# First row tile's scores by one 256-column matmul per component, and four moved positions in the order of the last two heads

## The chip, the cores and the metric

The kernel runs on one core of one Trainium2 chip. The metric is the device time of one execution in microseconds (us). Names of engines: PE is TensorE (matmuls), PEld its weight loads, DVE is VectorE, ACT is ScalarE, POOL is GpSimd, SP is SyncE, which only issues transfers.

## What is computed

One decoder block over 512 tokens of width 1024, in float32: differential attention with 8 heads (two score components of 64 dimensions each per head) beside a causal pooling branch, a gated merge, an output projection, and an MLP with squared ReLU. The change touches the attention scores:

```python
for i in range(S // Q_BLOCK):                 # four row tiles of 128 queries
    q0 = i * Q_BLOCK
    kend = q0 + Q_BLOCK
    s = jnp.einsum('bqhcd,bkhcd->bhcqk', qb, kb)          # c: two components
    s = jnp.where(mask, s, -jnp.inf)                      # causal
    p = jax.nn.softmax(s, axis=-1)
    w = p[:, :, 0] - lam * p[:, :, 1]
    outs.append(jnp.einsum('bhqk,bkhd->bqhd', w, vb))
```

Row tile i has 128 queries and (i + 1) * 128 keys, so the first row tile has 128 keys only.

## The kernel before

Everything is laid out with 128 partitions. Each float32 operand of a matmul is kept as a rounded high part and a low remainder (type fp32r), and a product is summed from the parts that matter. For the scores the high part of q and its remainder stand together in `qs[:, c]` (64 partitions each), the high part of k in `kz[:, c]` with the other 64 partitions zero, and `ks[:, c]` has k's remainder in one half and k's high part in the other. A row tile's scores of a component are then two matmuls with the same stationary operand, `qs` against `ks` (line 395) and `qs` against `kz` (line 396), summed in one PSUM bank.

The work goes in this order: the value projection (to 56 us), the eight heads (`attn`, 57 to 305 us), the output projection and the MLP. Within the heads the program calls `attn(h)`, then the q and k projection of the next head (`qk`), then some "fillers": input projections of the pooling branch (`pool(g)`, names u0 to u3) and of the gates (`gate`, names ga0 to gp7), and the merges. Every projection is 24 matmuls of 512 columns (`mm3`, lines 131, 132 and 135). Its sum lies in one of three PSUM banks, used in turn (`acc`); a new projection or pooling product (`pp`, lines 485 to 489) can start in a bank when DVE has read the bank's last sum. So u3, which comes three uses behind gp5 (gp5, pp4, pp5, u3), starts behind the DVE instruction that reads gp5 (line 474).

For each row tile of a head: scores (lines 395, 396), on DVE a mask with a row minimum (397), on ACT two exponentials (401), on DVE a reciprocal and a scaling (403, 404), on ACT a scaling (405), on DVE the difference of the components (406), on PE the transposes of the result (410), and then two copies into the buffer `wt` (412, 413). When all four row tiles are in `wt`, twelve matmuls multiply it by the values (418, called PV here). There is one `wt`, so that a head's copies wait for the PV matmuls of the head in front. Score banks are two, used in turn (`sbk`), and so are the banks of the transposes (`tbk`).

The program is not run in the order in which it is written: a scheduler with a cost model sorts the instructions of each engine ahead of time, within the dependencies. `after(later, earlier)` adds a dependency that holds `later` behind `earlier` in that order, with no semaphore. On the chip each engine takes its instructions strictly in that order.

Of the kernel before, what the change touches and what calls it, by code (L numbers as in the profile page):

```python
# [12 lines left out]
F32R = mybir.dt.float32r  # L13
I32 = mybir.dt.int32
AF = mybir.ActivationFunctionType
ALU = mybir.AluOpType
AX = mybir.AxisListType

P = 128
S = 512  # L20
D = 1024
NK = D // P
H = 8
# [4 lines left out]
NEG = -3.0e38  # L28
# [23 lines left out]
def block_kernel(ctx, tc, xT, x_tok, gains, pos, consts, w_in, w_v, w_pool, w_out, w_up, w_dn, out):  # L52
    nc = tc.nc
    V, A, G, T = nc.vector, nc.scalar, nc.gpsimd, nc.tensor
    EXPLN = "natural_log_exp_and_others"

    def after(later, earlier):
        tc.add_manual_dep(
            later.ins, earlier.ins.name,
            mybir.DependencyInfo(mybir.DependencyClass.NoSync, mybir.DependencyReason.DATA), reason="issue order",  # L60
        )

    state = {}
# [4 lines left out]
    cf = ctx1.enter_context(tc.tile_pool(name="cf", bufs=1))  # L68
    tp = ctx1.enter_context(tc.tile_pool(name="tp", bufs=1))
# [17 lines left out]
    def tmp(tag, name, shape=(P, S), dt=F32, bufs=2):  # L87
        return tp.tile(list(shape), dt, tag=tag, name=name, bufs=bufs)

    def f(ap):  # L90
        return ap.bitcast(F32)
# [35 lines left out]
    def mm3(acc, hi, lo, rh, rl):  # L127

        for k in range(NK):
            c = slice(k * P, (k + 1) * P)  # L130
            T.matmul(acc, lhsT=hi[:, c], rhs=rh[:, k, :], start=k == 0, stop=False)  # L131
            T.matmul(acc, lhsT=hi[:, c], rhs=rl[k], start=False, stop=False)  # L132
        for k in range(NK):
            c = slice(k * P, (k + 1) * P)
            T.matmul(acc, lhsT=lo[:, c], rhs=rh[:, k, :], start=False, stop=k == NK - 1)  # L135
# [19 lines left out]
    ident = cp.tile([P, P], F32, name="ident")  # L155
# [6 lines left out]
    mask = cf.tile([P, S], F32, name="mask")  # L162
# [15 lines left out]
    rb = cf.tile([P, S], F32, name="rb")  # L178
# [38 lines left out]
    for n in range(2):  # L217
        accs = [bank((0, 1, 2, 3, 4, 5, 6, 0)[4 * n + t], f"v{n}_{t}") for t in range(NT)]
        for kk in range(4):
# [24 lines left out]
            if n == 0 and 0 < kk < 3:  # L244
                i = kk - 1
# [111 lines left out]
    def proj(m, name, eng=None):  # L357
        hi, lo = get_w(w_in[m], name, eng)
        a_ = acc(name)
        mm3(a_, hi, lo, xh, xl)  # L360
        return a_

    lo_, hi_ = slice(0, 64), slice(64, 128)

    kzs = [cf.tile([P, 2, S], F32R, name=f"kz{i}") for i in range(2)]
    for kz in kzs:
        G.memset(f(kz)[hi_, 0, :], 0.0)
        G.memset(f(kz)[lo_, 1, :], 0.0)

    def qk(h):  # L370
        qs = tp.tile([P, 2, S], F32R, tag="qs", name=f"qs{h}", bufs=2)
        ks = tp.tile([P, 2, S], F32R, tag="ks", name=f"ks{h}", bufs=2)
        kz = kzs[h % 2]
        q = rope(proj(h, f"q{h}", V) if h else q0, f"q{h}")
        for c, own, oth in ((0, lo_, hi_), (1, hi_, lo_)):
            A.copy(out=qs[own, c, :], in_=q[own])
            V.tensor_tensor(out=qs[oth, c, :], in0=q[own], in1=f(qs)[own, c, :], op=ALU.subtract)
        k = rope(proj(8 + h, f"k{h}", V), f"k{h}")
        for c, own, oth in ((0, lo_, hi_), (1, hi_, lo_)):
            A.copy(out=kz[own, c, :], in_=k[own])  # L380
        for c, own, oth in ((0, lo_, hi_), (1, hi_, lo_)):
            A.copy(out=ks[oth, c, :], in_=f(kz)[own, c, :])
            V.tensor_tensor(out=ks[own, c, :], in0=k[own], in1=f(kz)[own, c, :], op=ALU.subtract)
        return qs, ks, kz

    def attn(h, qs, ks, kz):
        wt = wt_all
        for i in range(NT):
            N = (i + 1) * P
            qsl = slice(i * P, i * P + P)  # L390
            pr = tmp(f"p{i}", f"p{h}_{i}", (P, 2, N), bufs=1)
            st = tmp("st", f"st{h}_{i}", (P, 6), bufs=3)
            for c in range(2):
                s_ = sbk(f"s{h}_{i}_{c}")
                T.matmul(s_[:, :N], lhsT=qs[:, c, qsl], rhs=ks[:, c, :N], start=True, stop=False)
                T.matmul(s_[:, :N], lhsT=qs[:, c, qsl], rhs=kz[:, c, :N], start=False, stop=True)  # L396
                V.tensor_tensor_reduce(  # L397
                    out=pr[:, c, :N], in0=s_[:, :N], in1=mask[:, S - N :], scale=-0.125, scalar=-NEG,
                    op0=ALU.add, op1=ALU.min, accum_out=st[:, c : c + 1],
                )  # L400
                A.activation(out=pr[:, c, :N], in_=pr[:, c, :N], func=AF.Exp, scale=-1.0,  # L401
                             bias=st[:, c : c + 1], accum_out=st[:, 2 + c : 3 + c])
            V.reciprocal(out=st[:, 4:6], in_=st[:, 2:4])
            V.tensor_scalar(out=st[:, 5:6], in0=st[:, 5:6], scalar1=lvec, scalar2=None, op0=ALU.mult)
            A.activation(out=pr[:, 1, :N], in_=pr[:, 1, :N], func=AF.Copy, scale=st[:, 5:6])
            V.scalar_tensor_tensor(out=pr[:, 0, :N], in0=pr[:, 0, :N], scalar=st[:, 4:5], in1=pr[:, 1, :N],
                                   op0=ALU.mult, op1=ALU.add)
            t_ = tbk(f"t{h}_{i}")
            for j in range(i + 1):
                T.transpose(out=t_[:, j * P : j * P + P], in_=pr[:, 0, j * P : j * P + P], identity=ident)  # L410
            tv = t_[:, :N].rearrange("p (j q) -> p j q", q=P)
            A.copy(out=wt[:, 0, : i + 1, qsl], in_=tv)
            V.tensor_tensor(out=wt[:, 1, : i + 1, qsl], in0=tv, in1=f(wt)[:, 0, : i + 1, qsl], op=ALU.subtract)
        o_ = obk(f"o{h}")
        n = 0
        for vv, ww in ((vh, 0), (vl, 0), (vh, 1)):
            for j in range(NT):
                T.matmul(o_[:, j * P :], lhsT=vv[:, h, j * P : j * P + P], rhs=wt[:, ww, j, j * P :], start=n == 0, stop=n == 11,  # L418
                         skip_group_check=True)
                n += 1  # L420
        o = tmp("o", f"o{h}", bufs=2)
        A.copy(out=o, in_=o_)
        sqh = tmp("sqh", f"sqh{h}", dt=F32R, bufs=1)
        A.activation(out=sqh, in_=o_, func=AF.Square)
        sql = tmp("y", f"sql{h}", dt=F32R, bufs=1)
        sq = tmp("sq", f"sqo{h}")
        (V if h == H - 1 else G).tensor_tensor(out=sq, in0=o, in1=o, op=ALU.mult)
        (V if h == H - 1 else G).tensor_tensor(out=sql, in0=sq, in1=f(sqh), op=ALU.subtract)
        ss = obk(f"ss{h}")
        T.matmul(ss, lhsT=onesr, rhs=sqh, start=True, stop=False)  # L430
        T.matmul(ss, lhsT=onesr, rhs=sql, start=False, stop=True)
        y = tmp("y", f"y{h}", bufs=1)
        rsqrt(y, ss, sq, P)
        if h == H - 1:
            return o, y
        V.scalar_tensor_tensor(out=o, in0=o, scalar=subc, in1=y, op0=ALU.mult, op1=ALU.mult)
        return o, None

    def pool(g):
        w = WINDOWS[g]  # L440
        a_ = proj(24 + g, f"u{g}", "dma")
        pad = tmp("u", f"u{g}", (P, 16 + S), bufs=1)
        G.memset(pad[:, :16], 0.0)
        u = pad[:, 16:]
        V.tensor_tensor(out=u, in0=a_, in1=rb, op=ALU.mult)
        bufs_ = [tmp("pa", f"pa{g}", (P, 16 + S), bufs=1), tmp("pb", f"pb{g}", (P, 16 + S), bufs=1)]
        for b_ in bufs_[:g]:
            G.memset(b_[:, :16], 0.0)
        cur, s_ = pad, 1
        n = 0  # L450
        while s_ < w:
            nxt = bufs_[n % 2]
            G.tensor_tensor(out=nxt[:, 16:], in0=cur[:, 16:], in1=cur[:, 16 - s_ : 16 + S - s_], op=ALU.add)
            cur, s_, n = nxt, 2 * s_, n + 1
        win = cur[:, 16:]
        d = bufs_[n % 2][:, 16:]
        V.scalar_tensor_tensor(out=d, in0=win, scalar=1.0 / w, in1=u, op0=ALU.mult, op1=ALU.subtract)
        V.tensor_tensor(out=d[:, :w], in0=win[:, :w], in1=rcc[:, :w], op=ALU.mult)
        V.tensor_tensor(out=d[:, :w], in0=d[:, :w], in1=u[:, :w], op=ALU.subtract)
        dh = tmp("dh", f"dh{g}", dt=F32R, bufs=1)  # L460
        dl = tmp("dl", f"dl{g}", dt=F32R, bufs=1)
        A.copy(out=dh, in_=d)
        V.tensor_tensor(out=dl, in0=d, in1=f(dh), op=ALU.subtract)
        wr = tmp("wpr", f"wpr{g}", (P, 256), bufs=1)
        after(nc.sync.dma_start(out=wr, in_=w_pool[:, g, :]), state["x"])
        wph = wt_all[:, 0, 2, 0:256]
        wpl = wt_all[:, 1, 2, 0:256]
        A.copy(out=wph, in_=wr)
        V.tensor_tensor(out=wpl, in0=wr, in1=f(wph), op=ALU.subtract)
        return dh, dl, wph, wpl  # L470

    def gate(m, name, dst):
        a_ = proj(m, name, "dma")
        V.tensor_tensor(out=dst, in0=a_, in1=rb, op=ALU.mult)

    def merge(h, sg, a, sa, sp, dh, dl, wph, wpl):
        a, y = a
# [554 lines left out]
```

## Time and profile before

| | |
|---|---|
| median of 3 runs | 674.83 us (674.45 to 675.34) |
| the profiled execution | 674.09 us, span of the profile 671.9 us |
| PE busy | 663.1 us (99%), 3688 matmuls |
| DVE, ACT, POOL busy | 526.1, 461.0, 112.0 us |
| granted TensorE clock, mean of the core | 0.996 |

The profiled execution is 0.74 us below the median; 2.2 us of it lie outside the span. In the timeline of the profile a row has start, duration, engine, line, operation, the names out<-in, and the shape; the duration of a matmul runs to its modelled end and so overlaps the matmul behind it. What a matmul costs PE is therefore read here from the starts of two rows that follow each other.

### The profile page before, as it was taken

The page shows a single profiled execution, that of the slowest core. Times are in us where ns is not written, and L with a number is a line of the kernel's source. Part 1 is how long each engine was busy: PE and PEld are TensorE (multiplying, and loading weights), DVE is VectorE, ACT ScalarE, POOL GpSimd, SP SyncE. Part 2 cuts the span into 40 slices and gives each one's busy share as a digit, 9 for nine tenths or more (in the row PEclk, how much of TensorE's full clock was granted, in tenths as well). Part 3 has the DMA queues.
Part 4 walks back from the last instruction along what each step waited for, and adds up shares of the span by engine and source line. Part 5 has one row for each costly group of instructions (what it writes and reads, how often), then busy time and mean ns, then how long its engine had stood idle before and what let it go on. Part 6 is the DMA issues. An engine that isn't in the chain of part 4 may idle for free.

```text
span 671.9 us, 9994 instructions
## 1 busy us (share of the span) xinstructions
PE 663.1 (99%) x3688; PEld 579.6 (86%) x3688; DVE 526.1 (78%) x882; ACT 461.0 (69%) x741; POOL 112.0 (17%) x130
## 2 busy tenths in 40 slices
PE   9999999999999999999999999999999999999995
PEld 7888888888888888888889988999889998899884
DVE  6855977799979986875588998657994599747995
ACT  8465587978887698884477975367743695256974
POOL 2001110142133212520202020202102021210120
PEclk9999999999999999999999999999999999999998
DMA  9416464435263365574976596776959578494863
GB/s 317 162 57 185 126 151 126 103 94 126 87 142 103 98 166 105 126 184 172 312 208 112 159 235 186 167 191 146 236 199 187 193 164 261 117 212 132 214 126 125
DMA packets 32880, 109.34 MB, mean 163 GB/s; under 512 B 4032, under 2 KB 4928, under 8 KB 32832
## 3 DMA queue, kind: packets, MB, share of 16 engines
q0 software_dynamic: 10656, 38.80, 32.3%
q1 hardware_dynamic: 21744, 69.38, 29.3%
q8 instruction: 29, 0.48, 0.3%
q10 hardware_dynamic: 432, 0.52, 0.2%
q14 instruction: 19, 0.16, 0.1%
HBM read 106.59 MB, written 2.10 MB: 162 GB/s over the span
## 4 chain that ended last, share of the span: by engine, by line
PE 98%; DMA 1%; DVE 0%; ACT 0%; issue 0%; SPq 0%
PE um L785 8%; PE um L788 8%; PE um L782 8%; PE dm L875 8%; PE dm L877 8%; PE dm L878 8%; PE v L235 2%; PE o L418 2%; PE ga L132 2%; PE ga L131 2%; PE gp L135 2%; PE gp L132 2%; PE k L132 2%; PE k L131 2%; PE gp L131 2%; PE k L135 2%
## 5 line engine op out<-in xcount | busy, mean ns | idle before, releaser
L877 PE MATMUL dm<-wh_dt,z 128*128 128x512 f32 (+1 forms) x128 | 49.5, 386 | 0.0
L878 PE MATMUL dm<-wl_dt,z 128*128 128x512 f32 (+1 forms) x128 | 49.4, 386 | 0.0
L875 PE MATMUL dm<-wh_dt,z 128*128 128x512 f32 (+1 forms) x128 | 49.0, 387 | 0.0
L785 PE MATMUL um<-gss,wh_ut 128*128 128x256 f32 x192 | 48.2, 283 | 0.0
L782 PE MATMUL um<-gss,wh_ut 128*128 128x256 f32 x192 | 48.0, 283 | 0.0
L401 ACT ACTIVATE p<-p,st 128x128 f32<-128x128 f32 (+3 forms) x64 | 35.7, 558 | 14.1 <-DVE st L397 13.8
L895 DVE TENSOR_TENSOR x<-x,dm 128x512 f32<-128x512 f32 x48 | 32.5, 681 | 16.3 <-PE dm L878 16.3
L112 ACT CAST wh_ut<-wga_uNone 128x1024 fp32r<-128x1024 f32 x24 | 24.9, 1050 | 29.7 <-PE dm L877 19.2
L112 ACT CAST wh_ub<-wr_u 128x1024 fp32r<-128x1024 f32 x24 | 25.1, 1050 | 22.1 <-PE um L785 9.8
L686 POOL DMA_DIRECT2D wga_dNone<-w_dn x16 | 14.2, 885 | 154.2 <-DVE wl_dt L113 154.2
L113 DVE TENSOR_TENSOR wl_ut<-wga_uNone,wh_ut 128x1024 fp32r<-128x1024 f32 x24 | 29.1, 1221 | 13.0 <-ACT wh_ut L112 12.9
L877 PE MATMUL dm<-wh_db,z 128*128 128x512 f32 x96 | 37.2, 389 | 0.0
L878 PE MATMUL dm<-wl_db,z 128*128 128x512 f32 x96 | 37.2, 389 | 0.0
L785 PEld LDWEIGHTS um<-gss,wh_ut 128*128 128x128 f32 x192 | 36.9, 192 | 0.0
L782 PEld LDWEIGHTS um<-gss,wh_ut 128*128 128x128 f32 x192 | 36.8, 192 | 0.0
L875 PE MATMUL dm<-wh_db,z 128*128 128x512 f32 x96 | 35.7, 389 | 0.0
L113 DVE TENSOR_TENSOR wl_ub<-wr_u,wh_ub 128x1024 fp32r<-128x1024 f32 x24 | 29.1, 1219 | 7.4 <-ACT wh_ub L112 7.4
L686 POOL DMA_DIRECT2D wga_uNone<-w_up x18 | 15.6, 865 | 115.8 <-DVE wl_ut L113 81.4
L112 ACT CAST wh_dt<-wga_dNone 128x1024 fp32r<-128x1024 f32 x24 | 24.9, 1049 | 14.4 <-issue 6.7
L755 DVE TENSOR_TENSOR z<-rawz,z 128x1024 fp32r<-128x1024 f32 x28 | 33.6, 1218 | 0.5 <-ACT z L752 0.5
L397 DVE CUSTOM_DVE_ANT_0 p<-s,mask 128x128 f32<-128x128 f32 (+3 forms) x64 | 30.3, 484 | 3.6 <-PE s L396 3.5
L785 PE MATMUL um<-gab,wh_ub 128*128 128x256 f32 x128 | 32.5, 283 | 0.0
(324 smaller groups left out, 2203.3 us busy)
## 6 DMA issues: line engine op xcount, KB each, us to landing
wr_u<-w_up SPq DMA_DIRECT2D x24, 512.0 KB, 5.4
wr_d<-w_dn SPq DMA_DIRECT2D x24, 512.0 KB, 4.2
wga_uNone<-w_up POOLq DMA_DIRECT2D x18, 512.0 KB, 7.2
wga_dNone<-w_dn POOLq DMA_DIRECT2D x16, 512.0 KB, 5.7
wr_k<-w_in SPq DMA_DIRECT2D x8, 512.0 KB, 3.3
wr_ga<-w_in SPq DMA_DIRECT2D x8, 512.0 KB, 3.3
wr_gp<-w_in SPq DMA_DIRECT2D x8, 512.0 KB, 4.2
wl_ga<-w_in POOLq DMA_DIRECT2D x8, 512.0 KB, 5.4
```

Of the source, the lines that this page charges most:

```text
L112: ins = A.copy(out=hi[:, sl], in_=raw[:, sl])
L113: (eng or G).tensor_tensor(out=lo[:, sl], in0=raw[:, sl], in1=f(hi)[:, sl], op=ALU.subtract)
L131: T.matmul(acc, lhsT=hi[:, c], rhs=rh[:, k, :], start=k == 0, stop=False)
L132: T.matmul(acc, lhsT=hi[:, c], rhs=rl[k], start=False, stop=False)
L401: A.activation(out=pr[:, c, :N], in_=pr[:, c, :N], func=AF.Exp, scale=-1.0, bias=st[:, c : c + 1], accum_out=st[:, 2 + c : 3 + c])
L755: lo = V.tensor_tensor(out=z[:, 1], in0=r, in1=f(z[:, 0]), op=ALU.subtract)
L782: m = T.matmul(a_, lhsT=hi[:, c], rhs=rh[:, k, :], start=p + k == 0 and onto is None, stop=False, skip_group_check=True)
L785: T.matmul(a_, lhsT=hi[:, c], rhs=rl[:, k, :], start=False, stop=False, skip_group_check=True)
L788: m = T.matmul(a_, lhsT=lo[:, c], rhs=rh[:, k, :], start=False, stop=k == 3, skip_group_check=True)
L875: m = T.matmul(a_, lhsT=zh, rhs=hi[:, sl], start=p == 0 and start, stop=False, skip_group_check=True)
L877: T.matmul(a_, lhsT=zl, rhs=hi[:, sl], start=False, stop=False, skip_group_check=True)
L878: end = T.matmul(a_, lhsT=zh, rhs=lo[:, sl], start=False, stop=p == 3, skip_group_check=True)
```

## The change

It has two parts. In the first, `ks` and `kz` of a head become one tile `kk` with four rows of 512 columns (index 0 is `ks`, index 1 is `kz`). For the first row tile alone, one matmul per component takes the 128 columns of `ks` and the 128 columns of `kz` side by side as 256 moving columns; the two halves come out side by side in the bank and are no longer summed by the matmul. DVE gets a new instruction (line 401 of the changed kernel): it adds the mask to the first halves of both components (128x256) and writes that to `pr`; the masking instruction then takes `pr` in the place of the mask, and so adds the second half. Row tiles 1 to 3 keep their matmuls.

In the second, four positions are held by `after`: the last head's transposes of row tile 0 behind the last PV matmul of the head in front; head 6's transposes of row tile 2 and the last head's first score matmul of row tile 1 behind the sixth matmul of the projection u3; and on DVE the difference of row tile 2 of head 6 behind the instruction that reads gp5.

```diff
     def mm3 ...
-            T.matmul(acc, lhsT=hi[:, c], rhs=rl[k], start=False, stop=False)
+            m = T.matmul(acc, lhsT=hi[:, c], rhs=rl[k], start=False, stop=False)
+            if k == 2:
+                state["mm"] = m
...
-    kzs = [cf.tile([P, 2, S], F32R, name=f"kz{i}") for i in range(2)]
+    kks = [cf.tile([P, 2, 2, S], F32R, name=f"kk{i}") for i in range(2)]
...
     def qk(h):
-        ks = tp.tile([P, 2, S], F32R, tag="ks", name=f"ks{h}", bufs=2)
-        kz = kzs[h % 2]
+        ks, kz = (kks[h % 2][:, i] for i in range(2))
...
     def attn ...
+            if i == 0:
+                both = sbk(f"s{h}_0").rearrange("p (c k n) -> p c k n", c=2, k=2)
+                for c in range(2):
+                    T.matmul(both[:, c], lhsT=qs[:, c, qsl], rhs=kk[:, :, c, :P], start=c == 0, stop=True, skip_group_check=True)
+                diag = mask[:, S - P :].rearrange("p (o n) -> p o n", o=1).to_broadcast([P, 2, P])
+                V.tensor_tensor(out=pr, in0=both[:, :, 0], in1=diag, op=ALU.add)
             for c in range(2):
-                s_ = sbk(f"s{h}_{i}_{c}")
-                T.matmul(s_[:, :N], lhsT=qs[:, c, qsl], rhs=ks[:, c, :N], start=True, stop=False)
-                T.matmul(s_[:, :N], lhsT=qs[:, c, qsl], rhs=kz[:, c, :N], start=False, stop=True)
+                if i:
+                    s_ = sbk(f"s{h}_{i}_{c}")
+                    state["s", h, i, c] = T.matmul(s_[:, :N], lhsT=qs[:, c, qsl], rhs=ks[:, c, :N], start=True, stop=False)
+                    T.matmul(s_[:, :N], lhsT=qs[:, c, qsl], rhs=kz[:, c, :N], start=False, stop=True)
                 V.tensor_tensor_reduce(
-                    out=pr[:, c, :N], in0=s_[:, :N], in1=mask[:, S - N :], scale=-0.125, scalar=-NEG,
+                    out=pr[:, c, :N], in0=s_[:, :N] if i else both[:, c, 1], in1=mask[:, S - N :] if i else pr[:, c],
+                    scale=-0.125, scalar=-NEG,
...
+        if h == H - 1:
+            after(state["t", h, 0], state["o", h - 1])
...
     def pool(g):
+        if g == 3:
+            after(state["t", H - 2, 2], state["mm"])
+            after(state["s", H - 1, 1, 0], state["mm"])
...
     def gate ...
+        if name == "gp5":
+            after(state["p", H - 2, 2], ins)
```

With it the scheduler sorts the whole stretch of the heads anew. SP's order is the same row for row; POOL's differs in a few rows. Three places follow. In the rows a name has a running number (`s_0_0_626` is the bank of row tile 0, component 0; `ga_884` the sum of a gate's projection), and the last entry is the shape.

First, PE at the first head's row tile 0, before:

```order
L131 MATMUL ga_884<-xh,wh_ga_879 128x512
L395 MATMUL s_0_0_626<-ks_570,qs_569 128x128
L396 MATMUL s_0_0_626<-kz_563,qs_569 128x128
L132 MATMUL ga_884<-xlb,wh_ga_879 128x512
L395 MATMUL s_0_1_631<-ks_570,qs_569 128x128
L396 MATMUL s_0_1_631<-kz_563,qs_569 128x128
L131 MATMUL ga_884<-xh,wh_ga_879 128x512
```

and in the changed kernel (399 is the new matmul, 405 and 406 are the old lines 395 and 396):

```order
L131 MATMUL ga_880<-xh,wh_ga_875 128x512
L399 MATMUL s_0_625<-kk_563,qs_569 128x256
L405 MATMUL s_1_0_643<-kk_563,qs_569 128x256
L406 MATMUL s_1_0_643<-kk_563,qs_569 128x256
L399 MATMUL s_0_625<-kk_563,qs_569 128x256
L132 MATMUL ga_880<-xlb,wh_ga_875 128x512
```

Four matmuls of 128 columns have become two of 256, and the scores of row tile 1 have moved up between them.

Second, the start of u3, on PE, before (`gp_2611` is gp5, `t_2_2458` are the transposes of head 6's row tile 2, `s_0_0_2659` are scores of head 7, `u_2781` is u3; head 6's last score matmuls stand seven and eight rows above the first row shown):

```order
L431 MATMUL ss_2239<-sql_2235,onesr 128x512
L135 MATMUL gp_2611<-xh,wl_gp_2607 128x512 x8
L410 MATMUL t_2_2458<-ident,p_2_2442 128x128 x3
L395 MATMUL s_0_0_2659<-ks_2519,qs_2518 128x128
L396 MATMUL s_0_0_2659<-kz_564,qs_2518 128x128
L395 MATMUL s_0_1_2664<-ks_2519,qs_2518 128x128
L396 MATMUL s_0_1_2664<-kz_564,qs_2518 128x128
L131 MATMUL u_2781<-xh,wh_u_2776 128x512
```

and in the changed kernel (137 is the old 135, 447 the old 431):

```order
L405 MATMUL s_3_1_2450<-kk_563,qs_2231 128x512
L406 MATMUL s_3_1_2450<-kk_563,qs_2231 128x512
L137 MATMUL gp_2589<-xh,wl_gp_2585 128x512 x2
L399 MATMUL s_0_2637<-kk_564,qs_2497 128x256
L447 MATMUL ss_2221<-sql_2217,onesr 128x512
L399 MATMUL s_0_2637<-kk_564,qs_2497 128x256
L131 MATMUL u_2757<-xh,wh_u_2752 128x512
```

Between the last matmul of gp5 and u3 stood seven matmuls of 128 columns, and now stand two of 256 and one of 512; the last score matmuls of head 6 have moved to just ahead of gp5's end. DVE at the same place, before (397 masks, 474 reads gp5):

```order
L397 ISA p_3_2464,st_3_2465<-s_3_1_2471,mask 128x512
L397 ISA st_3_2465 128x1
L383 TENSOR_TENSOR ks_2519<-q1k_2592,kz_564 64x512 x2
L474 TENSOR_TENSOR g_2045<-gp_2611,rb 128x512
L397 ISA p_0_2657,st_0_2658<-s_0_0_2659,mask 128x128
```

and in the changed kernel (407 is the old 397, 493 the old 474, 417 the old 406, 426 the old 413):

```order
L407 ISA p_3_2443,st_3_2444<-s_3_1_2450,mask 128x512
L407 ISA st_3_2444 128x1
L493 TENSOR_TENSOR g_2029<-gp_2589,rb 128x512
L426 TENSOR_TENSOR wt<-t_1_2416,wt 128x2x128
L417 SCALAR_TENSOR_TENSOR p_2_2421<-p_2_2421,st_2_2422 128x384
L401 TENSOR_TENSOR p_0_2635<-s_0_2637,mask 128x256
```

The two subtractions of line 383 no longer stand between the masking of head 6's last scores and the reading of gp5, and the difference of row tile 2 (417) stands behind that reading.

Third, PE around head 6's PV matmuls, before (`t_0_2673` is the last head's row tile 0):

```order
L131 MATMUL gp_2868<-xh,wh_gp_2863 128x512
L410 MATMUL t_0_2673<-ident,p_0_2657 128x128
L132 MATMUL gp_2868<-xlb,wh_gp_2863 128x512
L135 MATMUL gp_2868<-xh,wl_gp_2864 128x512 x5
L418 MATMUL o_2487<-wt,vh 128x512
```

and in the changed kernel, where line 431 is PV and 421 the transposes:

```order
L431 MATMUL o_2466<-wt,vh 128x384
L431 MATMUL o_2466<-wt,vh 128x256
L431 MATMUL o_2466<-wt,vh 128x128
L421 MATMUL t_0_2649<-ident,p_0_2635 128x128
L421 MATMUL t_1_2669<-ident,p_1_2653 128x128 x2
```

The transpose of the last head's row tile 0 has moved behind the twelve PV matmuls, next to the two of row tile 1.

More of the change, by code (lines that the diff above doesn't have):

```diff
@@ L363, in block_kernel @@
     lo_, hi_ = slice(0, 64), slice(64, 128)
-    kzs = [cf.tile([P, 2, S], F32R, name=f"kz{i}") for i in range(2)]
-    for kz in kzs:
-        G.memset(f(kz)[hi_, 0, :], 0.0)
-        G.memset(f(kz)[lo_, 1, :], 0.0)
+    kks = [cf.tile([P, 2, 2, S], F32R, name=f"kk{i}") for i in range(2)]
+    for kk in kks:
+        G.memset(f(kk)[hi_, 1, 0, :], 0.0)
+        G.memset(f(kk)[lo_, 1, 1, :], 0.0)
     def qk(h):
         qs = tp.tile([P, 2, S], F32R, tag="qs", name=f"qs{h}", bufs=2)
-        ks = tp.tile([P, 2, S], F32R, tag="ks", name=f"ks{h}", bufs=2)
-        kz = kzs[h % 2]
+        ks, kz = (kks[h % 2][:, i] for i in range(2))
         q = rope(proj(h, f"q{h}", V) if h else q0, f"q{h}")
@@ L383, in qk, with attn @@
             V.tensor_tensor(out=ks[own, c, :], in0=k[own], in1=f(kz)[own, c, :], op=ALU.subtract)
-        return qs, ks, kz
-    def attn(h, qs, ks, kz):
+        return qs, kks[h % 2]
+    def attn(h, qs, kk):
+        ks, kz = (kk[:, i] for i in range(2))
         wt = wt_all
@@ L405, in attn @@
             A.activation(out=pr[:, 1, :N], in_=pr[:, 1, :N], func=AF.Copy, scale=st[:, 5:6])
-            V.scalar_tensor_tensor(out=pr[:, 0, :N], in0=pr[:, 0, :N], scalar=st[:, 4:5], in1=pr[:, 1, :N],
-                                   op0=ALU.mult, op1=ALU.add)
+            state["p", h, i] = V.scalar_tensor_tensor(out=pr[:, 0, :N], in0=pr[:, 0, :N], scalar=st[:, 4:5], in1=pr[:, 1, :N],
+                                                      op0=ALU.mult, op1=ALU.add)
             t_ = tbk(f"t{h}_{i}")
             for j in range(i + 1):
-                T.transpose(out=t_[:, j * P : j * P + P], in_=pr[:, 0, j * P : j * P + P], identity=ident)
+                turn = T.transpose(out=t_[:, j * P : j * P + P], in_=pr[:, 0, j * P : j * P + P], identity=ident)
+                if j == 0:
+                    state["t", h, i] = turn
             tv = t_[:, :N].rearrange("p (j q) -> p j q", q=P)
@@ L417, in attn @@
             for j in range(NT):
-                T.matmul(o_[:, j * P :], lhsT=vv[:, h, j * P : j * P + P], rhs=wt[:, ww, j, j * P :], start=n == 0, stop=n == 11,
+                m = T.matmul(o_[:, j * P :], lhsT=vv[:, h, j * P : j * P + P], rhs=wt[:, ww, j, j * P :], start=n == 0, stop=n == 11,
                          skip_group_check=True)
                 n += 1
+        state["o", h] = m
+        if h == H - 1:
+            after(state["t", h, 0], state["o", h - 1])
         o = tmp("o", f"o{h}", bufs=2)
@@ L473, in gate @@
         a_ = proj(m, name, "dma")
-        V.tensor_tensor(out=dst, in0=a_, in1=rb, op=ALU.mult)
+        ins = V.tensor_tensor(out=dst, in0=a_, in1=rb, op=ALU.mult)
+        if name == "gp5":
+            after(state["p", H - 2, 2], ins)
     def merge(h, sg, a, sa, sp, dh, dl, wph, wpl):
```

## The prediction

> **What bounds the kernel.** I read the page first: busy times, then the chain that ended last.
>
> ```profile
> span 671.9 us, 9994 instructions
> PE 663.1 (99%) x3688; PEld 579.6 (86%) x3688; DVE 526.1 (78%) x882; ACT 461.0 (69%) x741; POOL 112.0 (17%) x130
> PE 98%; DMA 1%; DVE 0%; ACT 0%; issue 0%; SPq 0%
> ```
>
> PE is busy for 99% of the span and carries 98% of the chain. A busy PE may still hide waits, since the ends of matmuls are modelled, so I asked next who waited: first for PE, then for its weight loads, where a wait shows if the matmul ahead is still drawn as running.
>
> ```profile
> PE warm L170 <- POOL eps L161: 1.1, 1, 1.1
> PE v L235 <- ACT wh_v L112: 0.5, 1, 0.5
> ...
> PEld u L131 <- DVE g L474: 0.2, 1, 0.2
> ```
>
> The first two lie in the first 6 us. In the stretch of the heads one wait for data is worth a line: u3 waits 0.2 us for DVE's reading of gp5. The windows then say how much room the others have there (columns: PE, PEld, DVE, ACT, POOL, granted clock, DMA share, GB/s):
>
> ```profile
> 57.00:305.00 248.00, 247.94 (x1195) 207.36 (x1194) 204.54 (x464) 195.95 (x361) 62.04 (x61) 1.00 0.52 129
> ```
>
> PE has no hole in these 248 us, the clock is full, DVE is busy for 82%. So time is worth what PE issues, plus what it waits; DVE's and ACT's work costs nothing until PE meets it.
>
> **The change part by part.** First what the four 128-column matmuls of a head cost PE now. Head 0:
>
> ```profile
> 80.84 0.39 PE L131 MATMUL ga<-xh,wh_ga 128*128 128x512 f32 x1
> 81.07 0.22 PE L395 MATMUL s<-ks,qs 128*128 128x128 f32 x1
> 81.13 0.27 PE L396 MATMUL s<-kz,qs 128*128 128x128 f32 x1
> 81.24 0.45 PE L132 MATMUL ga<-xlb,wh_ga 128*128 128x512 f32 x1
> 81.52 0.22 PE L395 MATMUL s<-ks,qs 128*128 128x128 f32 x1
> 81.58 0.28 PE L396 MATMUL s<-kz,qs 128*128 128x128 f32 x1
> 81.69 0.45 PE L131 MATMUL ga<-xh,wh_ga 128*128 128x512 f32 x1
> 81.98 0.40 PE L132 MATMUL ga<-xlb,wh_ga 128*128 128x512 f32 x1
> 82.21 0.39 PE L131 MATMUL ga<-xh,wh_ga 128*128 128x512 f32 x1
> ```
>
> From start to start a 512-column matmul between its like takes 0.23 us (80.84 to 81.07, 81.98 to 82.21). A pair of 128s takes 0.17 (0.06 and 0.11), and the 512 behind it takes 0.28 and 0.29 in the place of 0.23. That is the sign of something that a 128 is too short to cover: what stands behind it starts 0.11 us on from it, not 0.06, and the 512 behind the pair passes the shortfall on to the next. A pair costs 0.17 + 0.05 = 0.22 and 0.17 + 0.06 = 0.23, a head 0.45, eight heads 3.6 us. The Trainium skill (TensorE: Matmul & The Clock Gate, § LDWEIGHTS) gives the load of 128 weight columns as 128 / 1.2 = 107 ns, whatever the matmul's width; the 0.11 of this trace agrees with that.
>
> The upper bound is the place where four stand in a row, behind three transposes, ahead of u3:
>
> ```profile
> 263.76 0.49 PE L410 MATMUL t<-ident,p 128*128 128x128 f32 x3
> 264.01 0.31 PE L395 MATMUL s<-ks,qs 128*128 128x128 f32 x1
> 264.15 0.28 PE L396 MATMUL s<-kz,qs 128*128 128x128 f32 x1
> 264.26 0.28 PE L395 MATMUL s<-ks,qs 128*128 128x128 f32 x1
> 264.37 0.27 PE L396 MATMUL s<-kz,qs 128*128 128x128 f32 x1
> 264.71 0.50 PE L131 MATMUL u<-xh,wh_u 128*128 128x512 f32 x1
> 265.04 0.40 PE L485 MATMUL pp<-dh,wt 128*128 128x512 f32 x1
> ```
>
> From 264.01 to 264.71 are 0.70 us, of which 0.2 is the wait; 0.50, and the 512 behind takes 0.33, 0.10 over its usual: 0.60 for a head.
>
> Then what two 256-column matmuls cost. Row tile 1 has them in the trace, with the same operands:
>
> ```profile
> 86.08 0.39 PE L132 MATMUL q<-xla,wh_q 128*128 128x512 f32 x1
> 86.31 0.28 PE L395 MATMUL s<-ks,qs 128*128 128x256 f32 x1
> 86.42 0.28 PE L396 MATMUL s<-kz,qs 128*128 128x256 f32 x1
> 86.54 0.39 PE L131 MATMUL q<-xh,wh_q 128*128 128x512 f32 x1
> 86.77 0.28 PE L395 MATMUL s<-ks,qs 128*128 128x256 f32 x1
> ```
>
> Two take 0.23 (86.31 to 86.54), and the 512 behind them its usual 0.23: a 256 just covers the 0.11. So a head falls from 0.45 to 0.23, by 0.22, and in the case of four in a row from 0.60 to 0.23, by 0.37. Eight heads: 1.8 to 3.0 us. In the program's order most of the sixteen pairs stand like head 0's, alone or split between wide matmuls, one head has all four in a row and a few pairs stand by transposes, so I take 2.0, near the lower end. What is not in the trace is a moving operand that is read in two pieces of 128 columns. Bounds: a 256 in one piece, 0.115, and two 128s, 0.22 with what they leave behind; I take the first, since the count of columns and of weight loads is that of line 395's 256, and keep the second as a rival.
>
> A rule that speaks against this: the same page of the Trainium skill (§ Back-to-back issue gap) gives an isolated matmul N / 2.4 + 2.5 ns, 56 ns for 128 columns and 109 for 256; by it alone four of the one cost 223 and two of the other 218, and eight heads save 0.04 us. The rows above have 0.06 only for the first 128 of a pair; what it would make of the time is in rival (a).
>
> The new DVE instruction: 8 of 128x256 from PSUM, nearest rows:
>
> ```profile
> L397 DVE CUSTOM_DVE_ANT_0 p<-s,mask 128x512 f32<-128x512 f32 x16 | 10.9, 685 | 0.1
> L397 DVE CUSTOM_DVE_ANT_0 p<-s,mask 128x256 f32<-128x256 f32 x16 | 6.5, 419 | 2.7 <-PE s L396 2.7
> ```
>
> About 0.42 us each, 3.4 us of DVE in 248 us, from 82% to 84%. It also starts only when both components are there, and the masking behind it waits for it. I cost it at nothing: the cover is the distance between scores and transposes, which the order keeps wide (other projections stand between), and in the trace no transpose and no score bank makes PE wait for data. If the cover were gone, the price is 0.42 us a head.
>
> The transposes of the last head's row tile 0. Alone between 512s, as now:
>
> ```profile
> 283.19 0.27 PE L410 MATMUL t<-ident,p 128*128 128x128 f32 x1
> 283.22 0.48 PE L132 MATMUL gp<-xlb,wh_gp 128*128 128x512 f32 x1
> 283.54 1.31 PE L135 MATMUL gp<-xh,wl_gp 128*128 128x512 f32 x5
> 284.68 0.74 PE L418 MATMUL o<-wt,vh 128*128 128x512 f32 x4
> ```
>
> 0.03 and then 0.32 in the place of 0.23: 0.12 us. Next to row tile 1's two it costs one step in a row of 128s, 0.11. Nothing is gained on PE; what it does is that its two copies into `wt`, which wait for PV of head 6, cannot be reached by ACT and DVE too early. Behind it on PE are row tile 1's transposes, which stood behind PV before too. Zero. The holds on head 6's row tile 2 delay its transposes (now at 263.76, just ahead of u3) to behind u3's sixth matmul, with six pooling products between, some 3 us; PV of head 6, which needs them, starts at 284.68. Zero again. No transfer is moved: SP's order is the same, and POOL's moved rows are off the chain.
>
> Then u3, where the order does change a wait. Its first matmul waits for DVE's reading of gp5:
>
> ```profile
> 261.22 0.69 DVE L397 CUSTOM_DVE_ANT_0 p<-s,mask 128x512 f32<-128x512 f32 x1
> 261.82 0.09 DVE L397 DVE_READ_ACCUMULATOR2_ANT st<- 128x1 f32 x1
> ...
> 263.53 0.39 PE L135 MATMUL gp<-xh,wl_gp 128*128 128x512 f32 x1
> ...
> 263.96 0.69 DVE L474 TENSOR_TENSOR g<-gp,rb 128x512 f32<-128x512 f32 x1 [0.73 <-PE gp L135]
> 264.57 0.28 DVE L397 CUSTOM_DVE_ANT_0 p<-s,mask 128x128 f32<-128x128 f32 x1
> ```
>
> The last matmul of gp5 ends at 263.92, DVE starts 0.04 later, takes 0.69, and u3 starts 0.06 behind that (264.65 to 264.71). In the changed order count from the start of head 6's last score matmul (406 there). PE passes it (0.23), two of gp5 (0.46), a 256, a 512, a 256 (0.115 + 0.23 + 0.115) and stands at u3 after 1.15. DVE masks these scores from 0.39 + 0.04 = 0.43, the next instruction follows 0.60 on (261.22 to 261.82): gp5 is read from 1.03 to 1.72, u3 starts at 1.78. The wait is 0.63. If the masking didn't hold it, gp5's last matmul would: it starts at 0.46, ends at 0.85, the reading runs from 0.89 to 1.58, u3 at 1.64, a wait of 0.49. Against 0.2 now that is 0.3 to 0.4 more; I take 0.4.
>
> Sum: -2.0 + 0.4 = -1.6 us. The profiled execution's 674.09 would become 672.5; it lies 0.74 below the median of the runs, so on the median 674.83 becomes 673.2. Less than 0.2% (1.35 us) either way is about what a measurement of this kernel can't tell from no change, so -1.6 (-0.24%) stands just outside.
>
> **The rivals.** (a) Two 256s cost what four 128s do: because PE is paid by columns and the 0.11 behind a short matmul is only shifted (four times the 0.06 of a first 128 is 0.24, two 256s are 0.23), or because the two-piece operand streams no better than two 128s. Then the matmuls gain nothing and the wait at u3 stays: 674.83 + 0.4 = 675.2, no change. For it: no row shows such an operand. Against it: each pair's second step and the 512 behind it are longer in the rows, by 0.05 each, and that time is nowhere given back. (b) The gain comes, and part of it turns into new waits: a transpose or score bank that comes too early in a few heads, 0.3 to 0.4 us each at two or three places (the size of the wait at u3): 673.2 + 0.9 = 674.1, within 0.2%. For it: all heads are sorted anew by a cost model, and the one wait that I can work out grew. Against: now only one such wait stands in 248 us. (c) Slower: DVE becomes the bound in the heads, and the new instruction is paid in full by PE in each head: 8 x 0.42 = 3.4 on top of the forecast, 676.6. It decides from 7 of the 8 heads on (to be over 676.18 it needs 3.0 us, 7 x 0.42). For it: 84% busy is near the end. Against: DVE now waits for PE in this stretch (2.7 us at the 256-column masks alone), so it is ahead.
>
> **How the numbers follow.** The forecast 0.63, (a) 0.10, (b) 0.22, (c) 0.05. The forecast's own bounds: -3.0 + 0.3 gives 672.1, -1.8 + 0.4 gives 673.4. The range reaches down to 672.2 and up through (b) to 674.8, and leaves out (a) and (c), 0.15. Faster by over 0.2% (below 673.48) is the forecast, 0.63; within it (a) and (b), 0.32; slower 0.05.
>
> **What the profile after would show.** Matmuls 16 fewer; the new ones 0.11 to 0.12 us from start to start with 0.23 behind them (right) or 0.17 to 0.22 (rival a); u3's line among the weight loads' waits at 0.5 to 0.6 us; no further wait of PE or its weight loads between 57 and 305 us (b if there are); DVE's share of that stretch near 84%; u3's start and all behind it earlier by 1.6 us or so. I am wrong if the waits on transposes or score banks are more than 0.3 us in sum, or if the saving of a head is not near 0.22.

## The result: 0.2% slower, and the profile after

The changed kernel takes 675.76 us (median; 674.73 to 676.19), the kernel before on the same chip 674.27 (673.55 to 675.34): a ratio of 1.002, 95% interval 1.0014 to 1.0026, so 1.5 us slower where 1.6 us faster was forecast. The profiled execution took 675.78, its span 673.7. The page after, span, busy times and the chain that ended last:

```profile
span 673.7 us, 9969 instructions
PE 663.4 (98%) x3672; PEld 578.0 (86%) x3672; DVE 531.2 (79%) x890; ACT 458.4 (68%) x741; POOL 110.6 (16%) x130
PE 82%; DVE 6%; DMA 5%; ACT 3%; issue 3%; POOL 1%; SPq 0%; POOLq 0%; DVEq 0%; ACTq 0%
```

PE has its 16 matmuls fewer, and yet it no longer carries the chain alone (82% after 98%). The stretch of the heads says the same (columns as before: PE, PEld, DVE, ACT, POOL, clock, DMA share, GB/s):

```profile
57.00:305.00 248.00, 246.49 (x1173) 204.31 (x1172) 209.42 (x472) 193.28 (x359) 60.25 (x61) 1.00 0.52 127
```

PE has 1.5 us of holes here, where it had none; the clock is full. DVE is at 84%, as forecast. Who waits, PE first and then its weight loads:

```profile
PE s L405 <- DVE st L407: 1.2, 1, 1.2
...
PE u L131 <- DVE g L493: 0.3, 1, 0.3
...
PEld s L405 <- DVE st L407: 1.8, 2, 1.6
...
PEld t L421 <- DVE p L417: 0.5, 1, 0.5
PEld u L131 <- DVE g L493: 0.5, 1, 0.5
```

The wait at u3 was forecast. A wait of scores for a masking, over 1 us, and a wait of a transpose for the difference of the components (417) were not.

The matmuls themselves did what the prediction says. PE at head 0 (start, duration, engine, line, names, shape):

```profile
81.31 0.28 PE L399 MATMUL s<-kk,qs 128*128 128x256 f32 x1
81.42 0.29 PE L405 MATMUL s<-kk,qs 128*128 128x256 f32 x1
81.54 0.28 PE L406 MATMUL s<-kk,qs 128*128 128x256 f32 x1
81.66 0.28 PE L399 MATMUL s<-kk,qs 128*128 128x256 f32 x1
81.78 0.40 PE L132 MATMUL ga<-xlb,wh_ga 128*128 128x512 f32 x1
```

A 256 with a two-piece operand takes 0.11 and 0.12 from start to start, and the 512 behind it 0.24 (the next one starts at 82.02). Summed over all heads from such rows, the first row tiles' matmuls cost 3.95 us before (with what they leave to the 512 behind, without the wait at u3) and 1.9 now: 2.0 to 2.1 saved, 2.0 forecast.

The balance, each place read as the excess of a step between two PE rows over the usual step of that kind: 0.5 us at 155 to 157 us, 0.1 each at 130, 159 and 182, 0.3 at 226, 0.7 at u3 (264), 1.4 at 281, 0.3 at 375, about 3.6 in all before rounding, where before there were 0.25, at u3 alone. So -2.0 + 3.3, and 0.2 that PE already stands later at 33 us, make +1.5; the span grew by 1.8 and the medians by 1.5.

The largest wait, PE at 281 us:

```profile
281.17 0.39 PE L131 MATMUL gp<-xh,wh_gp 128*128 128x512 f32 x1
282.73 0.50 PE L405 MATMUL s<-kk,qs 128*128 128x512 f32 x1 [1.18 <-DVE st L407]
283.06 0.39 PE L406 MATMUL s<-kk,qs 128*128 128x512 f32 x1
```

The last head's scores of row tile 3, second component, need the bank that DVE's masking of row tile 2 empties. DVE's rows ahead of that masking, and POOL's at the same time:

```profile
277.68 1.29 DVE L514 TENSOR_TENSOR vl<-o,vh 128x512 fp32r<-128x512 f32 x1
278.89 1.52 DVE L208 SCALAR_TENSOR_TENSOR y<-sqo,y 128x512 f32<-128x512 f32 x1
...
280.41 1.79 DVE L417 SCALAR_TENSOR_TENSOR p<-p,st 128x128 f32<-128x128 f32 x1
282.12 0.55 DVE L407 CUSTOM_DVE_ANT_0 p<-s,mask 128x384 f32<-128x384 f32 x1
```

```profile
277.38 1.04 POOL L472 TENSOR_TENSOR pa<-u 128x512 f32<-128x512 f32 x1 [5.04 <-DVE u L464]
278.49 1.37 POOL L472 TENSOR_TENSOR pb<-pa 128x512 f32<-128x512 f32 x1
...
280.69 1.35 POOL L472 TENSOR_TENSOR pa<-pb 128x512 f32<-128x512 f32 x1
```

DVE was not idle there; three of its instructions took 0.6, 0.8 and 1.4 us longer than elsewhere, each while POOL's additions ran. The group of L417's 128-column form, before (there L406) and after, shows how a mean turns (xcount, busy us, mean ns):

```profile
L406 DVE SCALAR_TENSOR_TENSOR p<-p,st 128x128 f32<-128x128 f32 x8 | 2.8, 347 | 0.3 <-ACT p L405 0.3
```

```profile
L417 DVE SCALAR_TENSOR_TENSOR p<-p,st 128x128 f32<-128x128 f32 x8 | 6.1, 758 | 0.6 <-ACT p L416 0.5
```

The same eight instructions took 3.3 us more. A second place tells which instructions are hit. DVE, and then POOL, at 145 us:

```profile
144.52 0.69 DVE L407 CUSTOM_DVE_ANT_0 p<-s,mask 128x512 f32<-128x512 f32 x1
...
145.13 4.99 DVE L384 TENSOR_TENSOR kk<-q1k,kk 64x512 fp32r<-64x512 f32 x2
```

```profile
144.28 1.34 POOL L472 TENSOR_TENSOR pa<-u 128x512 f32<-128x512 f32 x1
145.35 1.51 POOL L503 TENSOR_TENSOR o<-o,g 128x512 f32<-128x512 f32 x1
146.60 1.25 POOL L472 TENSOR_TENSOR pb<-pa 128x512 f32<-128x512 f32 x1
147.59 1.25 POOL L443 TENSOR_TENSOR sqo<-o 128x512 f32<-128x512 f32 x1
```

The masking, whose scores come from PSUM, takes its usual 0.69 beside POOL's first addition. The two subtractions behind it read two SBUF tensors; their usual 0.69 each became 4.99 for both, and they ended only when POOL's run of four was over.

The places at 155 and 226 us look alike. DVE and POOL there, and one more wait of PE's weight loads:

```profile
153.74 1.78 DVE L417 SCALAR_TENSOR_TENSOR p<-p,st 128x512 f32<-128x512 f32 x1
```

```profile
153.25 1.72 POOL L444 TENSOR_TENSOR sql<-sqo,sqh 128x512 fp32r<-128x512 f32 x1
```

```profile
225.48 1.13 DVE L417 SCALAR_TENSOR_TENSOR p<-p,st 128x128 f32<-128x128 f32 x1
```

```profile
224.95 1.51 POOL L443 TENSOR_TENSOR sqo<-o 128x512 f32<-128x512 f32 x1 [1.58 <-ACT o L438]
```

```profile
PEld ss L447 <- POOL u L462: 0.2, 1, 0.2
```

L417 takes 0.75 us for 512 columns elsewhere and 0.35 for 128; the transposes of these results start at 155.67 and 226.66 us. The last line is another kind of wait: at 155.03 us the sum of squares waits for POOL's own result `sql`, of the instruction shown at 153.25, which took 1.72 us beside a DVE instruction with two SBUF inputs (L514, 153.13 us, its usual 0.69) and 1.29 where it is shortest. So POOL seems to be stretched by DVE too; no run here separates that. That wait costs PE some 0.1 of the 0.5 us at 155 to 157.

### The profile page after: what moved, and what is told of

It reads as the page before. It is cut to its first block, busy times and chain, and to the rows that moved or that the text cites. A ratio compares the mean times of both kernels' runs of the same rounds, so it can differ in the third digit from the quotient of the medians.

```text
span 673.7 us, 9969 instructions
## 1 busy us (share of the span) xinstructions
PE 663.4 (98%) x3672; PEld 578.0 (86%) x3672; DVE 531.2 (79%) x890; ACT 458.4 (68%) x741; POOL 110.6 (16%) x130
## 4 chain that ended last, share of the span: by engine, by line
PE 82%; DVE 6%; DMA 5%; ACT 3%; issue 3%; POOL 1%; SPq 0%; POOLq 0%; DVEq 0%; ACTq 0%
PE dm L898 7%; PE dm L896 7%; PE dm L899 7%; PE um L803 7%; PE um L806 7%; PE um L809 7%; DMA wga_uNone<-w_up 5%; PE v L237 2%; PE v L238 2%; PE v L239 2%; PE gp L137 2%; PE gp L132 2%; PE gp L131 2%; PE k L137 2%; PE o L431 2%
## 5 line engine op out<-in xcount | busy, mean ns | idle before, releaser
L113 DVE TENSOR_TENSOR wl_ut<-wga_uNone,wh_ut 128x1024 fp32r<-128x1024 f32 x24 | 28.9, 1223 | 13.3 <-ACT wh_ut L112 13.2
L707 POOL DMA_DIRECT2D wga_dNone<-w_dn x16 | 14.2, 885 | 152.3 <-DVE wl_dt L113 152.3
L113 DVE TENSOR_TENSOR wl_ub<-wr_u,wh_ub 128x1024 fp32r<-128x1024 f32 x24 | 29.1, 1220 | 7.7 <-ACT wh_ub L112 7.7
L806 PE MATMUL um<-gab,wh_ub 128*128 128x256 f32 x128 | 32.6, 284 | 0.0
L803 PE MATMUL um<-gab,wh_ub 128*128 128x256 f32 x128 | 32.4, 284 | 0.0
```

What stands on the lines that cost most here:

```text
L113: (eng or G).tensor_tensor(out=lo[:, sl], in0=raw[:, sl], in1=f(hi)[:, sl], op=ALU.subtract)
L707: return [G.dma_start(out=tiles[c], in_=src[q, b, c], accum_op=ALU.add) for c in range(2)]
L803: m = T.matmul(a_, lhsT=hi[:, c], rhs=rh[:, k, :], start=p + k == 0 and onto is None, stop=False, skip_group_check=True)
L806: T.matmul(a_, lhsT=hi[:, c], rhs=rl[:, k, :], start=False, stop=False, skip_group_check=True)
```

## The theory, its rivals and the experiments

Theory P: a DVE instruction with two SBUF inputs stands still while POOL reads SBUF, and the new order puts such instructions beside POOL's just ahead of work for which PE waits. The Trainium skill (SBUF — State Buffer, § SBUF: two separate sides) says so: DVE and GpSimd share a port pair as an exclusive lock, which a DVE instruction with two SBUF inputs needs, against a GpSimd instruction that reads SBUF, and the loser fully blocks. The rows above agree in that a DVE instruction ends only behind POOL's. Which of the two goes first they don't settle: at 281 us L417 starts 0.28 us ahead of POOL's addition (280.41 and 280.69) and is held all the same. POOL issues a transfer there as well, from 280.09 to 280.97; beside such an issue alone L417 takes its 0.35 (at 89.42 and 251.34 us), so that is not what holds it. Rival O: the order itself queues too much DVE work ahead of what PE needs, whatever POOL does. Further rivals stand with the runs.

Except in the two runs that are said to be sorted anew, every engine's order is held row for row, by dependencies without semaphores, as it is in the kernel named, apart from the rows that the text moves. Each was compared with the kernel before on its own chip (674.42, 674.34 and 674.28 us).

**POOL's reads taken away.** POOL's 26 elementwise instructions in the heads, here one of the four lines, write constants:

```diff
-            G.tensor_tensor(out=nxt[:, 16:], in0=cur[:, 16:], in1=cur[:, 16 - s_ : 16 + S - s_], op=ALU.add)
+            G.memset(nxt[:, 16:], 1.0)
```

> The changed kernel with every engine's order held as it is; only POOL's 26 elementwise instructions of 128x512 in the stretch of the heads (adds of the pooling branch, squares and their remainders, gate products) are replaced by constant fills of the same destination, so that POOL reads no SBUF there (their results are left out). Theory P: the matmuls did save 2.0 us, and 3 us of the 3.6 us of new waits of PE come from DVE instructions with two SBUF inputs that stand still while POOL computes; then most waits go, the one of u3 (0.6) stays, and the time is about 672.9 us, 1.4 below the kernel before. Rival O: the waits come from the new positions and from DVE's extra instruction themselves; then the time stays at 675.8, within 0.4.

Measured 672.93 us, ratio 0.9977 (0.9968 to 0.9987): P's number. One wait of PE in the heads is above 0.1 us, that at u3; and the two subtractions of 145 us, beside POOL's fills, are short again:

```profile
PE u L131 <- DVE g L497: 0.5, 1, 0.5
```

```profile
145.50 1.40 DVE L384 TENSOR_TENSOR kk<-q1k,kk 64x512 fp32r<-64x512 f32 x2
```

```profile
145.02 0.86 POOL L507 MEMSET o<- 128x512 f32 x1
145.49 0.86 POOL L476 MEMSET pb<- 128x512 f32 x1
```

POOL writes there without a break, and reads nothing. The fills are also shorter than what they replace (0.86 against 1.03 to 2.16 us) and wait for less, so this run takes away waits for POOL's own results too, such as the first at 155 us (0.1). The same edit to the kernel before is the control:

> The kernel before in its own order on every engine, but POOL's 26 elementwise instructions in the heads (squares, pooling adds, head products) write constants and read nothing; their results are left out. Theory P (POOL's reads only lengthen DVE's instructions, and that costs time only where PE stands right behind one): DVE's stretches, 14.2 us in the profile before, go, and yet PE had only the 0.2 us at u3 to lose, so 674.42 becomes 674.0 to 674.5. Rival R (POOL's reads slow PE's own operands or ACT too, so the 2.8 us that they cost the changed kernel are a tax on any order): 671.4 to 672.

Measured 674.24, ratio 0.9994 (0.9986 to 1.0003): no change. Its window:

```profile
57.00:305.00 248.00, 247.94 (x1198) 207.65 (x1197) 191.69 (x464) 196.06 (x360) 35.05 (x61) 1.00 0.50 129
```

DVE is busy for 191.69 us in the place of 204.54, 12.9 us less, and PE's 247.94 is the same to the hundredth. So POOL's reads are no tax on PE; they lengthen DVE, and that costs time only where PE stands right behind. Without them the change is worth 674.24 to 672.93, -1.3 us (on two chips), with its longer wait at u3 in it.

**Only the place at 281 us.** POOL's additions of the last pooling group alone write constants; there are four, the fourth at 284.67 us.

```diff
+            if g == 3:
+                G.memset(nxt[:, 16:], 1.0)
+            else:
                 G.tensor_tensor(out=nxt[:, 16:], ...)
```

> The changed kernel in its own order on every engine, but only the POOL adds of the last pooling group (three, at 277 to 282 us) write constants and read nothing; their result is left out. P: the DVE instructions at 277 to 282 us take their short times (the 128-column L417 0.35 in the place of 1.79 us, L208 0.7 in the place of 1.52), the 1.4 us wait of the last head's score matmul at 281 us goes or stays under 0.2, all other waits (155, 226, u3, 375) stay: 675.76 - 1.4 = 674.3. Rival O (the new order queues too much DVE work ahead of that masking, whatever POOL does): DVE has 0.3 us less at most, the wait stays at 1 us or more, 675.4 to 675.8.

Measured 673.99, ratio 0.9992 (0.9983 to 1.0001). The wait at 281 us is gone, those at 155, 226 and u3 stayed. DVE there:

```profile
278.26 0.68 DVE L208 SCALAR_TENSOR_TENSOR y<-sqo,y 128x512 f32<-128x512 f32 x1
...
278.94 0.33 DVE L417 SCALAR_TENSOR_TENSOR p<-p,st 128x128 f32<-128x128 f32 x1
```

O is out for this place: the same instructions in the same order, with four instructions of another engine that no longer read, and 1.8 us come back. P had 1.4; the 0.3 at 375 us, which this profile lacks too, would make up the rest, and why it is not there was not followed.

**The same place with nothing left out.** POOL's third addition (`add`) waits on a semaphore for the masking of row tile 2 (`state["m", H - 1, 2, 1]`):

```diff
+            if g == 3 and n == 2:
+                tc.add_manual_dep(add.ins, state["m", H - 1, 2, 1].ins.name, ...)
```

> The changed kernel in its own order on every engine, nothing left out; the one edit is a wait: POOL's third add of the last pooling group (280.69 us) starts only when DVE has done the masking L407 of the last head's row tile 2. P: with no POOL read beside it the 128-column L417 ahead of that masking takes 0.35 us in the place of 1.79, the score matmul's wait of 1.4 us at 281 us goes, and POOL's add comes some 0.5 us later than now, which nothing on PE waits for: 675.76 - 1.4 = 674.4, between 674.0 and 674.8. Rival L (the add stretches the next DVE instruction in the place of this one, and the last head's transposes, PV and squares wait later): half or more comes back, 675.1 to 675.8.

Measured 674.40, ratio 1.0001 (0.9993 to 1.001). DVE, POOL and PE:

```profile
280.97 0.32 DVE L417 SCALAR_TENSOR_TENSOR p<-p,st 128x128 f32<-128x128 f32 x1
```

```profile
281.93 1.41 POOL L472 TENSOR_TENSOR pa<-pb 128x512 f32<-128x512 f32 x1 [0.41 <-DVE st L407]
```

```profile
281.99 0.39 PE L405 MATMUL s<-kk,qs 128*128 128x512 f32 x1
```

One POOL instruction that waits 0.4 us took 1.4 us off the kernel, as P had it. That the number is met so closely is partly luck: in this profile the 0.3 at 375 us is gone as well, and some 0.35 came back at 295 us, where a sum of squares waits for POOL's `sql`, which took 2.16 us beside DVE's L113. The other remedy moves PE instead: the waiting score pair stands seven wide matmuls later (the order on PE, names and lines).

```diff
-s 405, 406
 gp 132, 131, 132, 131, 132, 131, 132
+s 405, 406
```

> The changed kernel in its own order, nothing left out, but the last head's score pair that waits 1.4 us at 281 us for DVE's masking stands seven wide matmuls (1.6 us) later on PE. P: PE does the seven in the time in which it stood, and the wait goes for nothing: 675.76 - 1.4 = 674.3, between 674.0 and 674.7. Rival L (the masking and exponential of these scores come later by as much, and the last head's transposes and PV wait in its place): 675.2 to 675.8.

Measured 675.53, ratio 1.0017 (1.0008 to 1.0025): P's number missed, L's right. (Its profiled execution, 677.41, is 1.9 us above the median and late by 2 us from the first norm on, so places are read from it, not the span.) In the place of the 1.4 us there are waits of the last head's followers, 0.6 at PV, 0.4 at a transpose (288.44 us), 0.3 at a sum of squares (297.40). The first:

```profile
286.00 0.86 PE L431 MATMUL o<-wt,vh 128*128 128x512 f32 x4 [0.29 <-ACT wt L425]
```

DVE was late here, and PE's distance alone does not bring its time back.

**The two parts of the change apart.** The holds alone, with the old matmuls, sorted anew:

```diff
+after(state["t", H - 1, 0], state["o", H - 2])
+after(state["t", H - 2, 2], state["mm"])
+after(state["s", H - 1, 1, 0], state["mm"])
+after(state["p", H - 2, 2], ins)
```

> The second part alone: the old score matmuls with the four holds, sorted anew. Theory P: no matmul saved; u3 waits 0.3 us longer, other waits by chance of the order: 674.3 to 675.0. If the holds are what costs the changed kernel (the wait of 1.5 us at the last head's last scores, 0.5 more at u3): 676.0 to 676.5.

Measured 674.70, ratio 1.0004 (0.9995 to 1.0013). One wait in the heads, u3's, 0.55 us where it was 0.25.

The matmuls alone, the changed kernel without these four lines, sorted anew:

> The first part alone, sorted anew by the scheduler, without the four holds. Theory P: the saving of 2.0 us less such waits as this order has; u3 no longer waits, but other places are open: 672.3 to 675. If the holds made the waits of 1.5 us at 281 us and 0.7 at u3: 673.5. Rival D: as the changed kernel, 675.8.

Measured 675.01, ratio 1.0009 (1.0 to 1.0017). The waits at 155 to 157, 182 and 226 us are those of the changed kernel, so they come with the first part's new order; in the place of 281's, the transposes ahead of u3, which the holds move away, wait:

```profile
265.33 0.55 PE L421 MATMUL t<-ident,p 128*128 128x128 f32 x3 [0.91 <-DVE p L417]
```

And the matmuls alone in the order of before, the new DVE instruction ahead of the first masking:

```diff
-s 395, 396 (128 columns, component 0)
+s 399, 399 (256 columns, components 0 and 1)
...
-s 395, 396 (128 columns, component 1)
```

> The first part alone (256-column score matmuls, the new DVE instruction), with every engine's order held as in the kernel before: both new matmuls stand where the first component's pair stood, the new DVE instruction directly ahead of the first masking of row tile 0. Theory P: the old distances are back, 2.0 us saved, u3's wait some 0.2 to 0.4: 672.3 to 672.9 us. Rival D (the new DVE instruction is paid by PE, 0.42 us in most heads): 674.3 - 2.0 + 3.4 = 675.7. Rival M (the matmuls save nothing): 674.3 to 674.6.

Measured 673.61, ratio 0.9991 (0.9981 to 1.0001): better than the re-sorted ones by 1.4, but short of what was expected. Three waits remain, 0.6 us at 215, 0.15 at 228.5 and 0.5 at u3. The first, on DVE, POOL and PE, is a DVE instruction beside POOL's again (usual: 0.75):

```profile
213.66 1.88 DVE L417 SCALAR_TENSOR_TENSOR p<-p,st 128x512 f32<-128x512 f32 x1
```

```profile
213.64 1.34 POOL L467 TENSOR_TENSOR pb<-pa 128x512 f32<-128x512 f32 x1
```

```profile
215.68 0.63 PE L421 MATMUL t<-ident,p 128*128 128x128 f32 x4 [0.41 <-DVE p L417]
```

But the kernel before has the same stretch at the same place, and PE lost nothing:

```profile
213.91 1.88 DVE L406 SCALAR_TENSOR_TENSOR p<-p,st 128x512 f32<-128x512 f32 x1
```

```profile
215.97 0.60 PE L410 MATMUL t<-ident,p 128*128 128x128 f32 x4
```

There the transposes start 0.23 behind the wide matmul ahead of them (215.74), which is PE's usual step: the cover was just used up. Up to here the new matmuls have brought PE 0.87 us ahead (the first matmul of this projection starts at 212.59, before at 213.46) and DVE only 0.25 (213.66, before 213.91). The difference, 0.62, is about the wait. So PE's saving itself takes cover away wherever DVE does not gain as much, in the old order too. This kernel without POOL's reads was not run.

**A version that beats both.** That kernel with three moves in PE's order:

```diff
-t 421 x4
 q 131, 132, 131, 132
+t 421 x4
...
-s 405, 406
 gp 131
+s 405, 406
...
-u3 131
 pp 499, 502, 503, 499, 502, 503
+u3 131
```

> The first part of the change alone in the order of before (the run that gave 673.61), and three moves on PE, nothing left out: the four transposes at 214.9 us stand four wide matmuls later, the score pair at 228.5 us one later, u3's first matmul behind the six pooling products. P: its waits of 0.56 + 0.03, 0.15 and 0.38 + 0.10 us are covered and nothing else is late: 673.61 - 1.2 = 672.4, between 672.1 and 672.8, some 2.0 below the kernel before. Rival L (what stands later is late for its own followers: the copies of the transposes and PV, u3's reading): half or more comes back, 673.0 to 673.6.

Measured 673.00, ratio 0.998 (0.9971 to 0.9989). The waits at 215, 228.5 and u3 are gone; 0.47 came back at 223 us, at a single transpose for which no POOL read is near:

```profile
223.21 0.33 PE L421 MATMUL t<-ident,p 128*128 128x128 f32 x1 [0.25 <-DVE p L417]
```

So half of 1.2. That transpose was moved behind the next score pair and one wide matmul:

```diff
-t 421
 s 405, 406
 k 132
+t 421
```

> The kernel that gave 673.0 (first part of the change in the order of before, three moves on PE), nothing left out, with one more move: the single transpose at 222.68 us, where PE waits 0.41 + 0.06 us, stands two score matmuls and one wide matmul later (0.58 us). P: the wait is covered, 673.0 - 0.45 = 672.5, between 672.2 and 672.8. Rival L (it comes back at the next transposes, as 0.41 of the 0.56 from 214.9 us did here): 672.9 to 673.2.

Measured 672.73, ratio 0.9984 (0.9975 to 0.9993), inside P's range, near its upper end, with u3 and all transposes covered; 0.3 us of wait came back, at the scores at 227.9 us, behind a masking that stands behind two DVE instructions stretched beside POOL's (L355 at 225.69 us: 1.77, usual 0.68). Both are faster than the kernel before by the whole of their intervals; from each other their intervals don't tell them apart.

## Why the prediction was wrong, by its steps

- **The matmuls: right.** -2.0 us forecast, 2.0 to 2.1 read from the rows, and the run without POOL's reads is 1.5 us below the kernel before on its chip (672.93 and 674.42), where 1.6 was forecast. Rival (a) is out.
- **u3: right in size.** 0.63 us forecast; u3's first matmul starts 0.54 later than its step allows and passes 0.10 on. The holds alone start it 0.55 late and the new matmuls alone, in the order of before, 0.38, against 0.23 in the kernel before, so the holds are not its only cause. Moved behind the six pooling products, in the better version, u3 no longer waits.
- **The new DVE instruction: right.** 0.42 forecast; eight at 416 ns, and DVE's share of the stretch 84%. Rival (c), that PE pays it in every head, is out: without POOL's reads it is there and no transpose waits. (Its seven heads come to 2.94 us, just under the 3.0 that it was said to need.)
- **The step that failed: "the cover is the distance between scores and transposes", costed at nothing, and with it "POOL's moved rows are off the chain".** No distance of the new order but u3's was worked out; the grounds were that the order keeps it wide and that no transpose or score bank waited in the profile before. But the duration of a DVE instruction with two SBUF inputs depends on what POOL does beside it: 0.35 or 1.79 us for one form. The new order brought such meetings ahead of scores and transposes at 155, 226 and 281 us; all three waits vanish when POOL's reads do, and at 281 us the wait also goes when nothing but POOL's time changes. This is rival (b) in kind (0.3 to 0.4 at two or three places, chance 0.22), but 2.8 us in size (675.76 to 672.93).
- **What the profile before had shown.** That no transpose and no score bank makes PE wait was true of PE's own rows, but not of its weight loads, where the prediction saw one wait for data in the heads. Their list has two more rows there, above the one of u3 and as long ("issue": nothing that the profile shows ended the wait):

```profile
PEld t L410 <- issue: 0.2, 1, 0.2
PEld s L395 <- DVE st L397: 0.2, 1, 0.2
```

They are a transpose (at 215.90 us, the place shown above) and scores behind a masking (at 218.89), the two kinds that grew. They cost PE nothing yet, but they say that no cover was left there. And one DVE and one POOL row, at 279 us:

```profile
279.05 2.33 DVE L206 SCALAR_TENSOR_TENSOR y<-sqo,y 128x512 f32<-128x512 f32 x1
```

```profile
279.24 1.58 POOL L453 TENSOR_TENSOR pb<-pa 128x512 f32<-128x512 f32 x1
```

A 0.69 us instruction took 2.33. DVE instructions stretched by over 0.15 us against the shortest of their form numbered 19 before (14.2 us in all) and 16 after (16.6); before, PE lost no time behind any of them, and at 215.97 us it stood right behind one. Busy shares gave no hint, since a blocked instruction counts as busy; the spread of one form's durations shows it.

What stays open: the 0.3 us at 375 us, in the MLP, which only the changed kernel's own profile has, and the 0.2 to 0.3 us by which the span grew beyond what the places add up to.

## What to carry to other kernels

Before costing a new order at nothing, list for each DVE form its shortest and longest duration, not the mean, and look at what POOL runs beside the long ones: an instruction with two SBUF inputs there must be priced at its stretched length wherever PE waits for what comes behind it. A saving on a saturated engine is safe only in an order whose covers were checked with these lengths; here the same saving was worth +1.5 us in the new order, -0.8 in the old one (an interval that just reaches no change) and -1.5 with four moves in that. The saving itself brings PE closer to what it waits for, so the covers are to be counted after it. Where a wait is DVE's lateness, look at the POOL instruction that blocks it as well as at the waiting matmul: at 281 us moving the first was worth 1.4 us and moving the second 0.2, while the wait at 215 us went by moving the transposes.

## What was not expected of the hardware

The block is not one POOL instruction long. POOL's four in a row at 144.28 to 148.84 us held two 0.69 us subtractions for 4.99 us (the first of them took 4.27): DVE did not get in between them, though it stood ready from 145.13 on. And the kind of operand decides, not the engine's load: beside POOL's reads, the 512-column maskings with scores from PSUM took 0.683 us on average against 0.685 alone (4 and 12 of them in the changed kernel's heads), the 128-column L417 with two SBUF inputs 1.44 against 0.35 (3 and 5).
